# A decoder trunk on one core: giving out the splits of the weights with a lead of 6.0 instead of 4.0

## The chip, the cores and the metric

The kernel runs on one core of a Trainium2 chip. The metric is the device time of one execution in microseconds (us). The core has a matrix engine (TensorE: PE in the profile, with PEld for its weight loads), VectorE (DVE), ScalarE (ACT), GpSimd (POOL), SyncE (SP, which only issues transfers here), and 16 DMA engines. Each engine has one stream of instructions and works through it in order; semaphores make one engine wait for another.

## What is computed

Two layers of a hybrid decoder on 256 tokens of width 1024, in fp32 (`rms_norm`, `swiglu` and the sub-layers are the usual ones):

```python
for l in range(2):
    h = h + 0.5 * swiglu(rms_norm(h, ffn1_norm[l]), ffn1_w_gate[l], ffn1_w_up[l], ffn1_w_down[l])
    h = h + hybrid_mixer(rms_norm(h, mix_norm[l]), w_in[l], ...)      # S5 scan beside differential attention
    h = h + memory_cross_attention(rms_norm(h, xattn_norm[l]), rms_norm(mem, mem_norm[l]),
                                   xattn_wq[l], xattn_wkv[l], xattn_wo[l])
    h = h + 0.5 * swiglu(rms_norm(h, ffn2_norm[l]), ffn2_w_gate[l], ffn2_w_up[l], ffn2_w_down[l])
return rms_norm(h, final_norm)
```

The mixer projects once (`w_in`) into the scan's input and q, k, v; it runs a complex diagonal scan over the 256 tokens with a gated output (`w_glu`), and causal differential attention with a bias; both halves go through `w_out`.

## The kernel before

**Weights in two parts.** Every product is made of three matmuls: high part of the activations by high part of the weights, high by low, low by high. So each weight tile is split on the chip. A unit is a 128 x 1024 tile of weights. SP loads it into one of `N_RAW` = 4 buffers (tile `raw`, in `fetch`, L578). ScalarE makes the high part (`whi`, times a gain where the norm's gain is folded in), VectorE the low part (`wlo` = raw times gain minus `whi`). `split_unit` (L582) does so for one half of 512 columns at a time, `split_whole` (L525) for all 1024 in ffn2. High and low parts have `N_W` = 5 buffers each.

**The list of units.** `stream_plan` (L104) lists all units in the order of use, with `need`, the time of each unit's first use on a clock that counts TensorE's ticks on weights alone: `STEP` = 1.28 per unit and token block, so 2.56 from unit to unit of a plain projection, which uses each unit for both blocks of 128 tokens at once. At the seams of sub-layers (ffn1 and ffn2 at their ends, w_glu, w_out, wq, wo) four units are held together: first all four for block 0, then all four for block 1, while block 0 is already being finished. In ffn2 pairs of chunks are made with seven products each in the manner of Strassen; such a unit ("S") is used for one STEP only.

**What sets the order.** The order of every engine's instructions is set when the program is written, by a planner: `Clock` (L168) carries `now`, the time of TensorE, and the times until which ScalarE, VectorE and GpSimd are occupied, by costs per instruction. The main program emits the matmuls on weights. Everything else (evacuations, attention, scan, tables) runs as tasks, Python generators, which are put in a heap with the time at which their input should be ready. Before every three matmuls on one half of a unit the main program calls `tick` (L618):

```python
def tick(self, ready):
    self.feed()
    self.c.run_due()
    self.c.now = max(self.c.now, ready + 0.13)
    self.main += STEP / 2
```

First `feed` (L503) emits splits, then `run_due` (L219) emits the tasks that are due, then `now` is moved to the time at which the planner has the half ready, then `main`, the place of the stream, moves by 0.64. `feed` goes on until a half is too far ahead or the buffers are used up:

```python
u, q = divmod(self.nsplit, 2)
if u >= self.nfree + N_W or (u > least and self.need[u] + q * STEP / 2 > self.main + LEAD):
    break
```

`split_next` (L515) also emits the loads: that of unit u + 4 behind the split of unit u.

**The mixer** (L1324). TensorE runs the four chunks of `w_in` (16 units), three chunks of `wkv` (12 units, products with the memory tokens, which depend on nothing in the layer and are there to fill the time), then `w_glu` and `w_out`. Beside the units run as tasks: `ssm_evac` (L1339), which copies the scan's input from PSUM (tile `z`) and changes its layout by four transfers issued on ScalarE's queue (tile `uq`); `ssm_states` (L1368), which reads `uq` into `up`, transposes it, and does the rotations and the scan on VectorE (tiles `p`); `attn` (L1478) for each token block, with its scores, maxima (`nm`) and sums on VectorE (tiles `sb`); and `ssm_out` (L1439), matmuls on the scan's result (`acc` from `W` and `p`). `w_glu` waits for its result.

Of the kernel before, what the change touches and what calls it, by code (L numbers as in the profile page):

```python
# [33 lines left out]
N_W = 5  # L34
N_S4 = 12
N_T5 = 3
LEAD = 4.0
STEP = 1.28
MARGIN = 0.2
BURST = 0.8  # L40
# [320 lines left out]
class Trunk:  # L361
# [141 lines left out]
    def feed(self, least=-1):  # L503
# [4 lines left out]
        while self.nsplit < 2 * n:  # L508
# [3 lines that stand above are left out]
# [1428 lines left out]
```

## Time and profile before

| | |
|---|---|
| median of 3 runs | 1204.16 us (1203.55 to 1204.84) |
| the profiled execution | 1206.8 us, its span 1203.7 us |
| TensorE matmuls busy | 1187.4 us (99%) |
| TensorE weight loads busy | 971.2 us (81%) |
| VectorE busy | 903.1 us (75%) |
| ScalarE busy | 711.2 us (59%) |
| bytes moved, mean rate | 210.91 MB, 175 GB/s |
| granted TensorE clock | 0.999 of full speed |

The profile is of one execution. Matmuls are pipelined, and their ends are modelled, so the distance between the starts of two matmuls tells more than their durations. A group of instructions carries the line of the helper that emits them (L345 matmuls, L356 transposes, L269 VectorE, L306 ScalarE), so groups are told apart by their tiles.

### The profile page before, as it was taken

To read this page: it belongs to the slowest core of one execution; us is meant where nothing else is said; L and a number is where in the kernel's file an instruction comes from. 1 tells how busy PE (TensorE), PEld (TensorE's weight loads), DVE (VectorE), ACT (ScalarE), POOL (GpSimd) and SP (SyncE) were. 2 spreads that over 40 slices of the span, in tenths; PEclk is the share of its full clock that TensorE was granted. 3 is DMA by queue.
4 is the path that set the end of the run, shared out by engine and by line. 5 is a ranking of instruction groups with operands and counts; after the bars stand their busy time and mean duration, and the time that the engine had idled before them with its cause. 6 is when DMAs were issued, how large, how long until landed. Compare 5 with 4: busy or idle time off the path is not lost.

```text
span 1203.7 us, 17730 instructions
## 1 busy us (share of the span) xinstructions
PE 1187.4 (99%) x6580; PEld 971.2 (81%) x6580; DVE 903.1 (75%) x1498; ACT 711.2 (59%) x1206; POOL 45.1 (4%) x104
## 2 busy tenths in 40 slices
PE   8999999999999999999999999999999999999997
PEld 7888888777888888888888888887678888888886
DVE  5797776498866688978668878565978576788885
ACT  6665455556856566555465544555687665556553
POOL 2100001000000000000010000100000000000000
PEclk9999999999999999999999999999999999999999
DMA  8656455544544566473556655655436455746542
GB/s 272 216 183 200 159 174 173 172 123 141 193 158 140 157 222 217 132 265 128 175 193 191 191 162 177 184 167 150 139 123 197 155 156 174 297 124 222 189 136 83
DMA packets 59974, 210.91 MB, mean 175 GB/s; under 512 B 7168, under 2 KB 8288, under 8 KB 59888
## 3 DMA queue, kind: packets, MB, share of 16 engines
q1 hardware_dynamic: 56304, 202.92, 51.8%
q0 software_dynamic: 2000, 5.24, 1.4%
q10 hardware_dynamic: 1584, 1.62, 0.5%
q8 instruction: 51, 0.84, 0.3%
q14 instruction: 35, 0.29, 0.1%
HBM read 207.00 MB, written 1.05 MB: 173 GB/s over the span
## 4 chain that ended last, share of the span: by engine, by line
PE 94%; DVE 2%; DMA 2%; ACT 1%; issue 1%; ACTq 0%; POOLq 0%; POOL 0%; DVEq 0%
PE mm L345 48%; PE acc L345 33%; PE tp L345 8%; PE tp L356 5%; DMA uq<-z 1%; DVE wlo L269 1%; DVE p L269 1%; DMA h<-in_x 0%; ACT whi L306 0%; DVE nm L269 0%; ACT junk L306 0%; ACT z L306 0%; ACT up L306 0%; ACTq L315 0%; DVE h L269 0%
## 5 line engine op out<-in xcount | busy, mean ns | idle before, releaser
L269 DVE SCALAR_TENSOR_TENSOR wlo<-raw,gains,whi 128x512 fp32r<-128x512 f32 x368 | 263.0, 747 | 92.2 <-ACT whi L306 90.7
L345 PE MATMUL mm<-whi,xh 128*128 128x512 f32 x768 | 307.0, 400 | 0.0
L345 PE MATMUL mm<-whi,xl 128*128 128x512 f32 x768 | 300.0, 391 | 0.0
L345 PE MATMUL mm<-wlo,xh 128*128 128x512 f32 x768 | 299.3, 390 | 0.3 <-DVE wlo L269 0.3
L306 ACT ACTIVATE whi<-raw,gains 128x512 fp32r<-128x512 f32 x368 | 240.8, 713 | 14.9 <-DMA raw<-in_wst 6.6
L345 PE MATMUL acc<-whi,gT 128*128 128x512 f32 (+1 forms) x712 | 238.9, 396 | 0.0
L269 DVE TENSOR_TENSOR wlo<-raw,whi 128x512 fp32r<-128x512 f32 (+1 forms) x236 | 209.7, 911 | 20.9 <-ACT whi L306 19.7
L306 ACT ACTIVATE whi<-raw 128x512 fp32r<-128x512 f32 (+1 forms) x236 | 180.9, 805 | 45.0 <-DMA raw<-in_wst 21.4
L345 PEld LDWEIGHTS mm<-whi,xh 128*128 128x128 f32 x768 | 144.5, 188 | 31.4 <-issue 1.3
L345 PEld LDWEIGHTS mm<-whi,xl 128*128 128x128 f32 x768 | 144.3, 188 | 30.6
L345 PEld LDWEIGHTS mm<-wlo,xh 128*128 128x128 f32 x768 | 144.8, 189 | 28.0 <-DVE wlo L269 0.6
L345 PEld LDWEIGHTS acc<-whi,gT 128*128 128x128 f32 x712 | 133.2, 188 | 26.3
L345 PE MATMUL acc<-wlo,gT 128*128 128x512 f32 (+1 forms) x356 | 138.0, 388 | 0.0
L345 PE MATMUL mm<-whi,mem 128*128 128x512 f32 x256 | 92.6, 410 | 0.0
L345 PEld LDWEIGHTS acc<-wlo,gT 128*128 128x128 f32 x356 | 67.1, 189 | 11.7
L306 ACT ACTIVATE sg<-mm,rstd 128x256 f32<-128x256 f32 x44 | 20.9, 474 | 85.5 <-PE mm L345 85.4
L306 ACT ACTIVATE gT<-tp 128x512 fp32r<-128x512 f32 x44 | 26.3, 598 | 56.4 <-PE tp L356 56.4
L306 ACT ACTIVATE z<-mm,rstd 128x256 f32<-128x256 f32 (+1 forms) x52 | 29.7, 571 | 49.6 <-PE mm L345 48.8
L345 PEld LDWEIGHTS mm<-whi,mem 128*128 128x128 f32 x256 | 48.1, 188 | 11.4 <-issue 1.3
L345 PE MATMUL mm<-wlo,mem 128*128 128x512 f32 x128 | 51.0, 398 | 3.9 <-DVE wlo L269 3.9
L306 ACT ACTIVATE xh<-tp 128x512 fp32r<-128x512 f32 x32 | 19.1, 596 | 59.6 <-PE tp L356 59.6
L269 DVE TENSOR_TENSOR gT<-tp,gT 128x512 fp32r<-128x512 f32 x44 | 30.2, 687 | 21.7 <-ACT gT L306 21.7
(256 smaller groups left out, 1539.9 us busy)
## 6 DMA issues: line engine op xcount, KB each, us to landing
raw<-in_wst SPq DMA_DIRECT2D x350, 512.0 KB, 4.0
blkX<-in_wst SPq DMA_DIRECT2D x8, 512.0 KB, 4.6
blkP<-in_wst SPq DMA_DIRECT2D x8, 512.0 KB, 8.1
blkY<-in_wst SPq DMA_DIRECT2D x8, 512.0 KB, 8.9
blkQ<-in_wst SPq DMA_DIRECT2D x8, 512.0 KB, 9.6
raw<-in_wst SPq DMA_DIRECT2D x4, 256.0 KB, 5.7
mem<-in_mem POOLq DMA_DIRECT2D x2, 512.0 KB, 7.4
uq<-z ACTq DMA_DIRECT2D x8, 128.0 KB, 4.7
```

The source lines that it names most:

```text
L269: r = getattr(self.e, name)(*a, **k)
L306: r = self.e.activation(out, in_, func, **k)
L345: r = self.e.matmul(out, lhsT, rhs, **k)
L356: r = self.e.transpose(out, in_, ident)
```

## The change

One constant of `feed` is changed: a half may be given out when it is needed within 6.0 of the stream's place instead of 4.0. The number of buffers, the list of units, the costs and everything else stay.

```diff
 N_W = 5
 N_S4 = 12
 N_T5 = 3
-LEAD = 4.0
+LEAD = 6.0
 STEP = 1.28
 MARGIN = 0.2
 BURST = 0.8
```

## Rows read from the trace of the kernel before

**Rows 1.** Page, part 1: engine, busy us, share of the span, instructions.

```profile
PE 1187.4 (99%) x6580; PEld 971.2 (81%) x6580; DVE 903.1 (75%) x1498; ACT 711.2 (59%) x1206; POOL 45.1 (4%) x104
```

**Rows 2.** Page, part 4: the chain that ended last, shares by engine.

```profile
PE 94%; DVE 2%; DMA 2%; ACT 1%; issue 1%; ACTq 0%; POOLq 0%; POOL 0%; DVEq 0%
```

**Rows 3.** Waits of TensorE, whole span: waited for, us in total, times, longest.

```profile
PE mm L345 <- DVE wlo L269: 4.2, 5, 1.4
...
PE tp L356 <- ACT up L306: 1.5, 2, 0.8
```

**Rows 4.** The same in two stretches: 262 to 275 us, then 855 to 868.

```profile
PE mm L345 <- DVE wlo L269: 2.0, 2, 1.4
...
PE mm L345 <- DVE wlo L269: 1.9, 2, 1.4
```

**Rows 5.** Windows view: stretch, length, then busy us and instructions of each engine.

```profile
241.00:292.00 51.00, 49.02 (x340) 36.39 (x338) 49.34 (x79) 31.17 (x70) 0.00 (x0) 1.00 0.44 135
```

**Rows 6.** Undisturbed matmuls (chain), then TensorE's timeline: start, us, instruction, count, [idle before].

```profile
316.52 16.33 PE acc L345 x72
...
264.81 0.62 PE L345 MATMUL mm<-whi,mem 128*128 128x512 f32 x2
...
267.17 0.62 PE L345 MATMUL mm<-whi,mem 128*128 128x512 f32 x2
...
269.22 0.62 PE L345 MATMUL mm<-whi,mem 128*128 128x512 f32 x2
...
270.21 0.63 PE L345 MATMUL mm<-whi,mem 128*128 128x512 f32 x2
...
272.28 0.62 PE L345 MATMUL mm<-whi,mem 128*128 128x512 f32 x2
...
273.81 0.63 PE L345 MATMUL mm<-whi,mem 128*128 128x512 f32 x2
...
275.66 0.39 PE L345 MATMUL mm<-wlo,mem 128*128 128x512 f32 x1
```

**Rows 7.** VectorE's timeline in the same stretch.

```profile
263.76 1.22 DVE L269 TENSOR_TENSOR p<-p,rot 128x1023 f32<-128x1023 f32 x1
...
266.03 0.75 DVE L269 SCALAR_TENSOR_TENSOR wlo<-raw,gains,whi 128x512 fp32r<-128x512 f32 x1
...
267.94 1.21 DVE L269 TENSOR_REDUCE nm<-sb 128x4 f32<-128x1024 f32 x1
269.07 1.41 DVE L269 SCALAR_TENSOR_TENSOR wlo<-raw,gains,whi 128x512 fp32r<-128x512 f32 x2
270.40 1.22 DVE L269 TENSOR_TENSOR p<-p,rot 128x1023 f32<-128x1023 f32 x1
...
272.67 2.07 DVE L269 SCALAR_TENSOR_TENSOR wlo<-raw,gains,whi 128x512 fp32r<-128x512 f32 x3
```

**Rows 8.** Timelines of VectorE and TensorE: two results and the instructions that use them.

```profile
276.03 0.35 DVE L269 SCALAR_TENSOR_TENSOR sb<-sb,sums 128x128 f32<-128x128 f32 x1
...
276.80 0.38 PE L356 MATMUL tp<-ident,sb 128*128 128x128 f32 x2
...
280.26 1.22 DVE L269 TENSOR_TENSOR p<-p 128x1023 f32<-128x1023 f32 x1
...
285.98 0.41 PE L345 MATMUL acc<-W,p 64*64 64x64 f32 x16
```

**Rows 9.** Chain of the stretch at the mixer's entry; then uq's times to landing.

```profile
218.83 1.93 ACT whi L306 x3
...
220.81 0.70 ACT z L306
...
222.14 6.22 DMA uq<-z
...
DMA to landing us min/median/max: 3.0/4.7/6.6
```

**Rows 10.** Page, part 6: issues, count, KB each, median us to landing.

```profile
raw<-in_wst SPq DMA_DIRECT2D x350, 512.0 KB, 4.0
```

## What to expect of it, worked out before it ran

> **What bounds the kernel now.** I read the page's busy shares first: TensorE has 1187.4 us of matmuls in a span of 1203.7 [rows 1]. The chain of work that ended last says the same from the other side: 94% of it is TensorE, 2% VectorE, 2% DMA [rows 2]. So whatever a change of order can give back is in the few places where TensorE waits. The waits of TensorE name them: 4.2 us for low halves of weights (tile wlo) in five waits, and 1.5 us for the tile up in two [rows 3]. Asked by stretch, four of the five waits for wlo are in two short stretches, one per layer, 2.0 and 1.9 us [rows 4]: the first units of wkv in the mixer, where VectorE also runs the scan of the SSM and the softmax of the attention. VectorE is busy for 49.3 of 51 us there [rows 5]. The late halves are not late because work is missing on ScalarE or from memory, but because they stand behind other instructions in VectorE's queue.
>
> **The change, part by part.** It removes and adds no instruction. The same units are loaded, split and multiplied; only the places in the instruction streams move. Four things move with LEAD.
>
> *When a half is given out.* feed issues half q of unit u at the first tick at which need[u] + 0.64 q is no more than main + LEAD, and main grows by 0.64 a tick. Units of a plain projection are four ticks apart. Counted from a unit's own first tick, its two halves are given out at ticks -6 and -5 with 4.0 (4.0/0.64 = 6.25) and at -9 and -8 with 6.0 (9.375): three ticks earlier. A tick is three matmuls; 72 of them take 16.33 us [rows 6], so 0.227 us each, 0.68 us a tick, 2.04 us for the three. Where a group of four is held for both token blocks, the limit of N_W = 5 buffers cuts this to about one to two ticks; the mixer's stretch is plain projections, so it gets all three.
>
> *What the late halves cost today.* Matmuls are paced by their starts, so I take starts, not the idle column, which misses part of it. Three matmuls take 0.68 us undisturbed. From the pair at 264.81 to the pair at 267.17 they took 2.36, from 269.22 to 270.21 0.99, from 272.28 to 273.81 1.53 [rows 6]. The excess is 1.68 + 0.31 + 0.85 = 2.84 us. The second layer repeats the pattern with a wait of 1.9 where this one has 2.0 [rows 4]; I take 2.8 for it too. Full removal is worth 5.6 us, and no more can come from this cause.
>
> *Whether three ticks are enough.* The three late halves are second halves of the first three wkv units. The first ends after the row at 266.03, behind two rotations of the scan that began at 263.76; the second is the first of the two at 269.07, behind a maximum that began at 267.94; the third is the first of the three at 272.67, behind two more rotations from 270.40 [rows 7]. Each was given out in the tick after, or a few ticks after, the scan step in front of it, so three ticks put it ahead of that step: 2.27 us earlier (263.76 to 266.03), 1.13 (267.94 to 269.07), 2.27 (270.40 to 272.67). Needed on a TensorE that never waited: about 1.7, 1.9 and 2.7. So at least the first is cured, the others nearly.
> The bound from below comes from the next unit. Its first half is the second of the three at 272.67 and ends near 274.1; it is used at 275.66 today [rows 6, 7], which would be 272.83 on a TensorE 2.83 us ahead. If it passes no scan step, 1.25 us of the gain is given back there, and a mixer yields 1.6. The bound from above is the full 2.8.
> I take 2.35 per mixer, nearer the upper end, for this reason: steps of the scan are put into the stream when the kernel's own clock says that the last one is done, and that clock is held up by a late weight (tick takes the weight's ready time into it). That it follows the chip through these waits is seen behind them: the first transposes of the attention's weights start at 276.80, 0.42 us after their input ends (276.03 + 0.35) [rows 8], although TensorE had lost 2.84 us just before. With less waiting, more ticks pass per scan step, and the next unit's halves pass the rotations too. Sum: 2 x 2.35 = 4.7 us.
>
> *What is pushed back instead.* The scan and the attention then finish later by what passed them: one and a half halves (three ticks of a half's two) and some two more where TensorE catches up, 0.7 us each by the spacing of the three at 272.67 [rows 7], so 1 to 2.5 us. The cover: the last rotation ends at 281.48 (280.26 + 1.22) and the matmuls on its result start at 285.98 [rows 8], 4.5 us; with TensorE 2.35 earlier and the scan 1 to 2 later it is nearly used up, not overdrawn. If it were gone, each us shows as a wait of the matmuls acc on W and p.
>
> *Queues that are passed.* ScalarE gives the high halves out three ticks earlier too; its evacuations (z, sg, xh, gT, qs) then stand behind up to two more halves, but most of them find ScalarE waiting for TensorE, so the halves fit into that idle time. SP's loads move with the splits: a slot is free earlier and its 512 KB, 4.0 us to landing [rows 10], are asked for earlier, at the same rate. The one DMA issue on ScalarE that matters is uq, below. POOL's few instructions are passed by nothing. All this I cost at 0, with plus or minus 0.7 us per mixer for uq (its wait today is 0.7 to 0.8 [rows 3]).
>
> *A rule that speaks against it.* TensorE's matmuls fill 99% of the span [rows 1]. The Trainium skill ("Perfetto Trace Analysis", Identifying the Most-Contended Engine) tells to improve the engine with the highest occupancy first; by that, reordering VectorE's queue would change nothing and the sum would be 0. The same section warns that the matmuls' busy share is a poor measure of TensorE. The starts above agree with the warning: inside rows that count as busy, 0.2 to 0.4 us per late half is lost beyond the idle column.
>
> **Against the runs.** The profiled execution took 1206.8 us, its span 1203.7. 1206.8 - 4.7 = 1202.1. That execution lies 2.6 above the median of the runs, 1204.16; on the scale of the medians the forecast is 1199.5. Differences under 0.2%, 2.4 us, can't be told from no change.
>
> **The rivals.**
> *The wait moves.* If the order on TensorE around the scan and the attention stays as it is, TensorE comes to the transposes of sb 2.8 us earlier, and these have 0.42 us to spare [rows 8]; 2.4 of 2.8 us come back as waits there. Gain 0.4 per mixer: 1203.4, at worst 1204.2. For it: VectorE has hardly a free microsecond [rows 5], so somebody has to be late. Against it: that clock reacts, and the streams have other units to run meanwhile.
> *The change doesn't do what it says.* The halves are given out earlier but VectorE's order in the crowded stretch stays, since scan steps come in blocks of two and a shift of three ticks may fall between two blocks; and elsewhere five buffers cap it. Then nothing moves: 1204.2, within 0.5. For it: one of the three late halves passes only 1.13 us of work. Against: the other two pass 2.27.
> *Slower: the exchange uq.* At the mixer's entry the chain runs through ScalarE: halves whi from 218.83, the copy z at 220.81, then the transfer uq from 222.14, 6.22 us long [rows 9], and TensorE waits for up at its end. It has no cover at all: every microsecond later goes through from the first one on. Two more halves in front of z cost 1.3 us (1.93/3 each) [rows 9]; one more weight load in front of uq costs up to the 4.0 us that a load takes to land [rows 10]. Both together are 5.3 us per mixer, 10.6 in all: 1204.16 - 4.7 + 10.6 = 1210.1. It ends above 1206.6 from 3.6 us per mixer on. For it: uq's time to landing already spreads from 3.0 to 6.6 us [rows 9]. Against: by the tick count only three or four halves fall between the two copies z instead of four, and the last copy waits for TensorE anyway.
> The Trainium skill says ("DMA: Bandwidth & Descriptors", Issuing engines are not separate DMA queues) that transfers from all issuing engines run on the same 16 DMA engines and interleave; by that uq is slowed by the weight loads beside it. The spread of uq agrees with it, though it doesn't prove it.
>
> **How the numbers follow.** Forecast 0.58, at 1199.5; its own range is 1204.16 - 5.6 - 0.8 = 1197.8 to 1204.16 - 3.2 + 0.8 = 1201.8. The wait moves 0.17, at 1203.4. Nothing changes 0.11, at 1204.2. Slower through uq 0.14, at 1210, the near end of it at 1206.6. The range of 1197.8 to 1206.2 leaves out most of the last case and some hundredths below. Faster by over 0.2% is the forecast but for its upper edge, 0.57; the same is the two middle cases and that edge, 0.29; slower is 0.14.
>
> **What would show it.** Right: TensorE's waits for wlo between 262 and 275 and between 855 and 868 fall from 2.0 and 1.9 us to under 0.5; in VectorE's timeline of that stretch the second half of the first wkv unit stands ahead of the two rotations; the last rotation ends a little later against the start of wkv; the rest of the span is as long as it was. Wrong: the waits for wlo are gone and as much appears at the transposes of sb or the matmuls on W (the wait moved); VectorE's order is unchanged (no effect); or the stretch from the copy z to up is longer by some us (uq). A gain over 6 us would mean that weights were late in places that the waits don't show.

## The result, and the profile after

The changed kernel takes 1213.24 us (median of 4 runs, 1212.84 to 1214.25) where the kernel before took 1204.12 beside it: a ratio of 1.0077, 95% interval 1.0064 to 1.0090, so 9 us slower. The forecast was 1199.5. The profiled execution took 1213.41, its span 1211.6 against 1203.7, 7.9 us more, at a granted clock of 0.997 against 0.999.

The first and the fourth part of the page after (busy time of each engine; shares of the chain that ended last), which answer [rows 1, 2]:

```profile
PE 1188.9 (98%) x6580; PEld 971.5 (80%) x6580; DVE 904.1 (75%) x1498; ACT 710.7 (59%) x1206; POOL 44.7 (4%) x104
...
PE 91%; ACT 4%; DVE 2%; issue 2%; DMA 1%; POOL 0%; ACTq 0%; POOLq 0%; DVEq 0%
```

Every count of instructions is what it was. Busy time is the same within 1.5 us on every engine. What changed is the chain: TensorE has 3% less of it, ScalarE 4% instead of 1%. TensorE's waits after (waited for, us in total, times, longest), which answer [rows 3]:

```profile
PE tp L356 <- DVE vl L269: 4.2, 4, 1.5
PE tp L345 <- DVE yT L269: 3.7, 2, 1.8
PE mm L345 <- DVE z L269: 2.4, 4, 0.8
PE tp L356 <- DVE prob L269: 2.0, 2, 1.0
...
PE mm L345 <- DVE wlo L269: 0.3, 1, 0.3
```

The waits that the change aimed at are gone: wlo fell from 4.2 to 0.3, and none is left in the two stretches of [rows 4] (the 0.3 is in the opening, at 14.9 us, and was there before); the two waits for up [rows 3] are gone too. In their place stand four others, each once or twice per layer, and none of them is on a weight. They are on results that VectorE makes: yT (the scan's output, at 304 and 900 us), vl (w_out's input behind its gate, four times), prob (the cross attention's weights, at 393 and 991) and z (in ffn2, four times).

Measured as the prediction measured, by the distance between the starts of neighbouring matmuls beyond their usual distance (0.227 us for 128 x 512), the ledger of the span is:

| place | before | after |
|---|---|---|
| wlo in wkv, two layers | 5.6 | 0 |
| up, two layers | 1.8 | 0 |
| yT | 0 | 4.0 |
| vl | 0 | 4.9 |
| prob | 0 | 2.3 |
| z in ffn2 | 0 | 3.1 |

About 7.4 us were gained and 14.3 lost, in places that the prediction didn't look at. Two more items belong to the sum: the opening is 1.0 us shorter in this execution (the 100th matmul starts at 24.84 us, and at 25.81 before), and the clock cost 1.7.

**A price behind a wait.** In the second layer the granted clock falls right behind the wait for yT, which ended at 902.51. The windows view (stretch, length, busy us and instructions of PE, PEld, DVE, ACT and POOL, granted clock, DMA share, GB/s):

```profile
902.83:906.25 3.42, 3.42 (x16) 3.02 (x14) 2.40 (x4) 0.35 (x1) 0.00 (x0) 0.50 0.60 207
```

0.50 is the lower of TensorE's two levels, 1.2 GHz. Matmuls of 128 x 512 start 0.43 us apart there (904.54 and 904.97) instead of 0.227, so half of the 3.42 us, 1.7, is lost. Ahead of the fall TensorE had stood for 1.83 us. The first layer's wait, just as long, was followed by no fall, and the kernel before has no such stretch between its opening and its last matmul. So a wait can cost more than its own length.

**Where a new wait comes from.** VectorE's and TensorE's timelines, kernel after (start, us, instruction, count, [idle before and what ended it]), around prob, then around yT and z:

```profile
391.89 1.89 DVE L269 TENSOR_TENSOR wlo<-raw,whi 128x512 fp32r<-128x512 f32 x3 [0.66 <-ACT whi L306]
...
393.89 0.62 DVE L269 TENSOR_SCALAR prob<-prob,sums 128x256 f32<-128x256 f32 x2
...
394.39 0.63 PE L356 MATMUL tp<-ident,prob 128*128 128x128 f32 x4 [1.00 <-DVE prob L269]
...
303.43 0.74 DVE L269 SCALAR_TENSOR_TENSOR wlo<-raw,gains,whi 128x512 fp32r<-128x512 f32 x1
304.10 1.28 DVE L269 TENSOR_TENSOR wlo<-raw,whi 128x512 fp32r<-128x512 f32 x2
305.30 1.06 DVE L269 TENSOR_TENSOR yT<-tp,yT 128x512 fp32r<-128x512 f32 x1
...
306.41 1.16 PE L345 MATMUL tp<-z,aT 128*128 128x128 f32 x8 [1.83 <-DVE yT L269]
...
434.79 2.36 DVE L269 TENSOR_TENSOR wlo<-raw,whi 128x1024 fp32r<-128x1024 f32 x2 [0.47 <-ACT whi L306]
437.06 0.48 DVE L269 SCALAR_TENSOR_TENSOR z<-mm,rstd,z 128x256 f32<-128x256 f32 x1
```

Three halves of wo stand ahead of prob, 1.89 us of work that is not needed yet, while TensorE stands for prob. The kernel before has the same instructions the other way round:

```profile
391.86 0.62 DVE L269 TENSOR_SCALAR prob<-prob,sums 128x256 f32<-128x256 f32 x2
392.38 1.89 DVE L269 TENSOR_TENSOR wlo<-raw,whi 128x512 fp32r<-128x512 f32 x3
```

At yT it is a late half of wkv (gains) and two halves of w_glu (no gains), at z two units of ffn2. At vl there is one step more; ScalarE's, VectorE's and TensorE's timelines, kernel after:

```profile
320.36 2.70 ACT L306 ACTIVATE whi<-raw,gains 128x512 fp32r<-128x512 f32 x4 [1.61 <-PE acc L345]
...
324.37 0.63 ACT L306 ACTIVATE gt<-gt 128x512 f32<-128x512 f32 x1
...
325.65 1.41 DVE L269 SCALAR_TENSOR_TENSOR wlo<-raw,gains,whi 128x512 fp32r<-128x512 f32 x2 [1.76 <-ACT whi L306]
326.98 0.68 DVE L269 TENSOR_TENSOR vl<-vl,gt 128x512 f32<-128x512 f32 x1
...
330.02 0.63 PE L356 MATMUL tp<-ident,vl 128*128 128x128 f32 x4 [1.54 <-DVE vl L269]
```

ScalarE first stands 1.61 us, until matmuls of TensorE end, before it can make four high halves; the sigmoid gt, which vl needs, waits behind them and a table load of 1.28 us; on VectorE two more halves stand ahead of vl. ScalarE's idle time ahead of whi, by what ended it (us, times), gives the size of that for the whole kernel, first before, then after:

```profile
  PE acc L345: 17.0, 13
...
  PE mm L345: 4.1, 4
```

```profile
  PE acc L345: 55.6, 27
  PE mm L345: 18.0, 13
```

21.1 us before, 73.6 after. Nothing but a buffer can make a split wait for a matmul, since its input comes from memory: `feed` counts a buffer as free when its last matmul has been emitted, and a half given out that early stands at the head of ScalarE's queue until the chip has done that matmul. Whatever is queued behind it stands too. That this costs TensorE time is tried in the third experiment.

### The profile page after: what moved, and what is told of

It is laid out like the page before. It is cut to its first block, busy times and chain, and to the rows that moved or that the text cites. A ratio compares the mean times of both kernels' runs of the same rounds, so it can differ in the third digit from the quotient of the medians.

```text
span 1211.6 us, 17723 instructions
## 1 busy us (share of the span) xinstructions
PE 1188.9 (98%) x6580; PEld 971.5 (80%) x6580; DVE 904.1 (75%) x1498; ACT 710.7 (59%) x1206; POOL 44.7 (4%) x104
## 4 chain that ended last, share of the span: by engine, by line
PE 91%; ACT 4%; DVE 2%; issue 2%; DMA 1%; POOL 0%; ACTq 0%; POOLq 0%; DVEq 0%
PE mm L345 47%; PE acc L345 31%; PE tp L345 8%; PE tp L356 5%; DVE wlo L269 1%; ACT whi L306 1%; ACT junk L306 1%; ACT L306 1%; DMA h<-in_x 0%; ACT xh L306 0%; DMA raw<-in_wst 0%; DVE vl L269 0%; ACT yg L306 0%; DVE yT L269 0%; POOL rstd L329 0%
## 5 line engine op out<-in xcount | busy, mean ns | idle before, releaser
L306 ACT ACTIVATE whi<-raw,gains 128x512 fp32r<-128x512 f32 x368 | 243.6, 714 | 45.5 <-PE acc L345 32.1
L269 DVE SCALAR_TENSOR_TENSOR g<-mm,rstd,sg 128x256 f32<-128x256 f32 x44 | 21.1, 481 | 39.3 <-ACT sg L306 39.3
```

The costliest lines, as they stand in the source:

```text
L269: r = getattr(self.e, name)(*a, **k)
L306: r = self.e.activation(out, in_, func, **k)
```

## The experiments

The theory after the result: the halves of the *next* group stand ahead of evacuations for which TensorE is about to wait (order), and a part of it is ScalarE standing for a buffer (buffers). Rivals: the mixer itself pays, because the scan was pushed back; or the earlier transfers disturb. In each experiment but the third, fourth and sixth, `feed` takes the lead from a function of the unit's group, and the diff shows that function, with its constants written out (from the seventh on against the function of an earlier experiment):

```diff
-self.need[u] + q * STEP / 2 > self.main + LEAD
+self.need[u] + q * STEP / 2 > self.main + lead_of(self.plan[u])
```

Times are medians beside runs of the kernel before on the same chip (1204.2 to 1204.8).

**1. The mixer's stretch alone.**

```diff
+def lead_of(p):
+    return 6.0 if p[0] == "w_in" or (p[0] == "wkv" and p[2] < 12) else 4.0
```

> The lead of 6.0 for the mixer's projections alone (w_in and the three chunks of wkv in it), 4.0 for all other units. What the comparison of the traces suggests: the longer lead takes away the waits of TensorE for wlo in wkv (5.6 us by starts, both layers) and for up (1.8), and the new waits (yT 4.0, vl 4.9, prob 2.3, z 3.1 us by starts) each have halves of the NEXT group's units in front of them: w_glu before yT, w_out and wq before vl, wo before prob, ffn2 before z. By that theory this run keeps the gain and drops vl, prob and z: 1196.5 to 1201 us, the upper end if yT's wait stays. The rival, that the shift of the mixer itself sets its tail off balance (TensorE comes out of wkv 8 us earlier than before, at results that are no earlier), gives waits for yT and vl here too: 1203 to 1208 us.

Measured: 1197.64 us, ratio 0.9937 (0.9920 to 0.9954); span 1197.2. TensorE's waits have one new row, for yT (1.3 us, twice, 0.7 at most), and none for vl, prob, z, up. So the change is worth 6.5 us of span (7.2 by the medians) where the prediction looked, even more than forecast, and the wait for yT, 0.8 us per layer by starts, is all that the scan's tail pays for it.

**2. All but the mixer's stretch.**

```diff
+def lead_of(p):
+    return 4.0 if p[0] == "w_in" or (p[0] == "wkv" and p[2] < 12) else 6.0
```

> The complement: 4.0 for w_in and the mixer's wkv, 6.0 for all other units. Theory of the next group's halves: waits for wlo in wkv are back (5.6 us), vl, prob and z stay (10.3 us), yT with them in part: 1212 to 1219 us. Rival (mixer off balance): prob and z stay (5.4 us), vl and yT go: 1207 to 1211 us.

Measured: 1215.92 us, ratio 1.0090 (1.0075 to 1.0105); span 1213.8. TensorE's waits:

```profile
PE mm L351 <- DVE wlo L275: 4.1, 5, 1.4
PE tp L362 <- DVE vl L275: 2.8, 4, 0.8
PE mm L351 <- DVE z L275: 2.4, 4, 0.8
PE tp L362 <- DVE prob L275: 2.0, 2, 1.0
```

The waits of before are back (up, with 1.3, is further down), and vl, z and prob are there without the mixer: the loss comes from the other groups. A wait for g in the opening, 1.8 us, is in this run and not in the whole change. The halves don't add: -6.5 and +10.1 us of span make +3.6, the whole made +7.9. By starts and without the first 25 us, where the opening differs, the gap is 5.3 us, and three items make it up: yT loses 2.0 us per layer by starts in the whole change and 0.8 in the first experiment, vl's first wait 1.7 against 1.0 in this one, and the clock cost 1.7 in the whole and nothing in either half. At a seam, halves of both groups meet.

**3 and 4. Buffers or order.** Six buffers for the parts, while `feed` is still held to five units, so that no half is given out earlier; the space comes from N_S4 (another pool, 12 to 10). The control has the smaller pool alone. Both have the lead 6.0 everywhere.

```diff
 N_W = 5
+N_BUF = 6
-N_S4 = 12
+N_S4 = 10
...
-        self.hip = P("hi", N_W)
-        self.lop = P("lo", N_W)
+        self.hip = P("hi", N_BUF)
+        self.lop = P("lo", N_BUF)
```

> Lead 6.0 everywhere, halves given out by the same limits (five units), but six buffers each for high and low parts, paid for with two of the twelve general tiles (10 instead of 12). With the longer lead ScalarE stands at a split whose buffer TensorE has not left for 89 us instead of 27, and holds what is behind it. If these stand-stills cause the new waits (theory of the buffers), they go here: 1199 to 1206 us. If only the place in the queue counts (a half in front costs its own 0.7 us on ScalarE and on VectorE, waiting or not), the time stays at that of the changed kernel: 1211 to 1215 us.

> Control for the run with six buffers: lead 6.0, five buffers, ten general tiles instead of twelve. Both theories: the changed kernel's time within 1.5 us, 1211.5 to 1215 us; if it is slower, that is the price of the two tiles and is to be taken off the run with six buffers.

Measured: six buffers 1208.24 us, ratio 1.0031 (1.0020 to 1.0042), span 1206.0; the control 1213.62, ratio 1.0071 (1.0056 to 1.0086), span 1210.5, with the waits of the changed kernel. Neither profile has a stretch at the lower clock in mid-span, so the 4.5 us between the two spans hold nothing of the clock. TensorE's waits, and ScalarE's idle time for TensorE ahead of whi, six buffers:

```profile
PE tp L346 <- DVE yT L270: 3.7, 2, 1.8
PE mm L346 <- DVE z L270: 2.4, 4, 0.8
PE tp L357 <- DVE prob L270: 2.0, 2, 1.0
...
PE tp L357 <- DVE vl L270: 0.5, 2, 0.2
```

```profile
  PE acc L346: 5.4, 10
```

With a buffer to spare ScalarE stands 5.4 us instead of 73.6, and vl falls from 4.9 us by starts to 0.8. yT, z and prob keep their size to a tenth. So about 4 us of the loss is ScalarE standing for buffers, and it shows at vl alone; the other 9.4 us (4.0 + 2.3 + 3.1) stay, and by the timelines above they are plain order on VectorE. The fifth experiment tries that.

**5. Three groups put back to 4.0.** w_glu, wo and ffn2 go back to 4.0; w_in, wkv, wq, w_out and ffn1 keep 6.0.

```diff
+def lead_of(p):
+    return 4.0 if p[0] in ("w_glu", "wo", "ffn2_gu", "ffn2_dn") else 6.0
```

> Lead 6.0, but 4.0 for the units of w_glu, wo and ffn2, whose halves stand in front of yT, prob and z in the changed kernel. Theory of the place in the queue: these three waits go (4.0 + 2.3 + 3.1 us by starts), vl stays (4.9), since it hangs on the buffers: 1213.3 - 9.4 = 1203.9, so 1202 to 1206 us. Rival (the waits come from TensorE's being early at the mixer's tail, and from ScalarE's time in general): yT or prob stay for the most part: 1207 to 1211 us.

Measured: 1203.74 us, ratio 1.0000 (0.9990 to 1.0009); span 1201.9. prob (wo stood ahead of it) and z (ffn2) are gone, vl is unchanged at 4.2, a wait for g in the opening has 1.3, yT is down from 3.7 to 1.3, as in the first experiment. Each of the three waits goes, or shrinks to what the first experiment has, with the group whose halves stand ahead of it.

**6. A lead of 5.0 everywhere.**

```diff
-LEAD = 6.0
+LEAD = 5.0
```

> Half of the change: lead 5.0 everywhere. By the rounding to ticks a half of a plain projection is given out one tick earlier than with 4.0 (at -7 for -6), not three. If gain and loss both grow with the lead step by step: TensorE's waits for wlo in wkv fall by about half (2 to 3 us less), and part of the new waits (vl, yT, prob, z) is there, 3 to 7 us: 1204 to 1209 us. If the loss sets in at once where halves come to stand in front of an evacuation, it is all there already: 1210 to 1214 us.

Measured: 1215.66 us, ratio 1.0093 (1.0078 to 1.0108); span 1214.4. Halfway between is slower than either end, for two reasons of its own. The first is a wait for z, once per layer, 8.9 us in total. ScalarE's timeline and TensorE's:

```profile
290.48 1.28 ACT L306 ACT_TABLE_LOAD   x1
291.77 1.09 ACT L306 ACTIVATE yg<-acc 128x512 f32<-128x512 f32 x2
...
295.10 1.28 ACT L306 ACT_TABLE_LOAD   x1
296.40 0.51 ACT L306 ACTIVATE sb<-sb,nm 128x256 f32<-128x256 f32 x1
...
301.28 1.23 ACT L306 ACTIVATE z<-mm,rmem 128x512 f32<-128x512 f32 x2
...
301.99 0.79 PE L345 MATMUL mm<-whi,mem 128*128 128x512 f32 x1 [4.43 <-ACT z L306]
```

Here the scan's gelu (yg) has come to stand ahead of the exponentials of the attention's second block (sb) on ScalarE, with a table load of 1.28 us ahead of each; in the kernel before the exponentials come first (290.27) and one load (294.84) lies between them and yg. All this, and yT, stands ahead of z, which frees the PSUM tile that TensorE needs: ScalarE works without a pause from 288.85 to the end of z. There are 13 table loads in the kernel where before and after have 11. The second reason is the clock. It is at its lower level at both waits, for 6.83 us from 301.19 and for 3.41 from 901.93, which is worth 5.1 us; all four runs have a mean clock of 0.993 to 0.995. By this estimate 5.0 would take about 1210.5 us at the full clock, and 6.0, without its 1.7, about 1211.5. The lead doesn't only shift halves: it changes which ticks pass while a task waits, and with that the order of the tasks among each other.

**7 and 8. Other leads around a mixer at 6.0.** First everything else at 3.0, then w_glu alone at 3.0 with the rest at 4.0.

```diff
 def lead_of(p):
-    return 6.0 if p[0] == "w_in" or (p[0] == "wkv" and p[2] < 12) else 4.0
+    return 6.0 if p[0] == "w_in" or (p[0] == "wkv" and p[2] < 12) else 3.0
```

```diff
 def lead_of(p):
+    if p[0] == "w_glu":
+        return 3.0
     return 6.0 if p[0] == "w_in" or (p[0] == "wkv" and p[2] < 12) else 4.0
```

> Lead 6.0 for the mixer's projections, 3.0 for all others (two ticks less than before). Outside of the mixer the weights had 1.1 us or more to spare with 4.0 except at the first units of ffn2 (0.4 to 0.6 us). If a shorter lead only takes spare time away, little changes or waits for wlo at the groups of four appear: 1197 to 1201 us. If evacuations still stand behind halves at 4.0, less lead is a gain: 1195 to 1197 us.

> Lead 6.0 for the mixer's projections, 3.0 for w_glu, 4.0 for the rest: the run with the mixer alone, but with w_glu's halves moved further back from yT. If the wait for yT that is left there (0.8 us by starts in each layer) comes from w_glu's halves in front of it, it goes: 1195.5 to 1197 us; if from TensorE's earlier arrival, nothing moves: 1197 to 1198.5 us.

Measured: 1207.32 us, ratio 1.0025 (1.0015 to 1.0036), and 1201.01 us, ratio 0.9973 (0.9962 to 0.9984). Both are slower than expected. A shorter lead brings weights late: with 3.0 the matmuls of w_glu wait 1.8 us for wlo in both, and with 3.0 everywhere there are 2.1 us more of waits for wlo in other groups and 0.9 for z in ffn2. The wait for yT (1.3) doesn't move with w_glu's lead: without w_glu's halves it is one half of wkv itself that stands ahead of yT (302.67 and 303.33 on VectorE).

**9. The mixer's wkv alone.**

```diff
 def lead_of(p):
-    return 6.0 if p[0] == "w_in" or (p[0] == "wkv" and p[2] < 12) else 4.0
+    return 6.0 if p[0] == "wkv" and p[2] < 12 else 4.0
```

> Lead 6.0 for the mixer's three chunks of wkv alone, 4.0 for w_in and the rest. The run with w_in and wkv at 6.0 won 7.2 us and lost the waits for wlo in wkv (5.6 us by starts) and for up (1.8). If the wait for up goes by w_in's halves being out of the way of the copy z and the transfer uq, it is back here: 1198.5 to 1200.5 us. If it went for another reason, 1197 to 1198.5 us.

Measured: 1203.49 us, ratio 0.9992 (0.9983 to 1.0002); span 1201.3. Neither expectation held. The waits for wlo are mostly gone, as expected, but the wait for up stays, and yT is larger than in the first experiment:

```profile
PE tp L362 <- DVE yT L275: 3.3, 2, 1.6
PE tp L362 <- ACT up L312: 1.7, 2, 1.3
```

**10. w_in and two of the three chunks of wkv.** If the half ahead of yT is one of the last chunk, that chunk should go back to 4.0.

```diff
 def lead_of(p):
-    return 6.0 if p[0] == "w_in" or (p[0] == "wkv" and p[2] < 12) else 4.0
+    return 6.0 if p[0] == "w_in" or (p[0] == "wkv" and p[2] < 8) else 4.0
```

> Lead 6.0 for w_in and the first two chunks of wkv, 4.0 for the third chunk and the rest. With all three chunks at 6.0 one wait for yT of 0.8 us per layer is left, behind one half of wkv's last unit on VectorE. If that half is the cause, the wait goes and the time falls by 1 to 1.6 us: 1195.8 to 1197 us. If TensorE only comes too early there, it stays: 1197.2 to 1198.5 us.

Measured: 1196.85 us, ratio 0.9937 (0.9920 to 0.9953); span 1195.0, the shortest of all. All of TensorE's waits:

```profile
PE pz L351 <- DVE zero L275: 1.2, 1, 1.2
PE tp L362 <- DMA h<-in_x: 0.7, 1, 0.7
PE mm L351 <- DVE wlo L275: 0.3, 1, 0.3
```

What is left lies in the first 16 us. Against the first experiment its time is not distinguishable: the medians differ by 0.8 us, and of the 2.2 us between the profiled spans 1.7 lie in the opening, where the two kernels give out the same halves (its wait for wlo ends at 16.24 us in the first experiment and at 14.54 here).

The wait for yT is gone, but not for the reason expected. Two halves of wkv still stand just ahead of yT on VectorE (from 303.46 us; yT starts at 304.78). What has changed is TensorE's order: the second group of transposes of yg starts 4.8 us behind the first (301.68 and 306.45) and not 1.14 us behind it (303.04 and 304.18 in the first experiment), so matmuls on wkv lie between the two. The expected time came by another way than the expected one, and whether the half of the last chunk was the cause stays open.

**11 and 12. Its two parts, each alone.** What does w_in's lead do, and do the parts add?

```diff
 def lead_of(p):
-    return 6.0 if p[0] == "w_in" or (p[0] == "wkv" and p[2] < 8) else 4.0
+    return 6.0 if p[0] == "w_in" else 4.0
```

```diff
 def lead_of(p):
-    return 6.0 if p[0] == "w_in" or (p[0] == "wkv" and p[2] < 8) else 4.0
+    return 6.0 if p[0] == "wkv" and p[2] < 8 else 4.0
```

> Only the units of w_in are given out with 6.0, everything else with 4.0. In e8 (the mixer's wkv alone with 6.0) TensorE's wait for up was still there, 0.6 and 1.4 us by starts, while with w_in at 6.0 too it is gone. Theory that the longer lead of w_in itself removes it: the wait for up is gone here (-1.8 us), the four waits for wlo in wkv stay (5.6 us by starts), no wait for yT, vl, prob or z beyond those of before: 1202.4, range 1201.6 to 1203.4. Rival, that the wait for up goes only when w_in and wkv are moved together: up stays, 1204.2.

> Only the first two chunks of the mixer's wkv are given out with 6.0, w_in and the rest with 4.0. Theory that the parts add: against the version with w_in and two chunks (1196.85) it misses what w_in's lead gives, the wait for up (2.0 us in e8) and 0.9 us of wlo at wkv's first unit: 1199.8, range 1199 to 1200.8, with no wait for yT, since the third chunk's halves stand where they stood. Rival, that the waits for yT in e8 (3.6 us) came from w_in at 4.0 beside wkv at 6.0 and not from the third chunk: they stay, 1203.4.

Measured: 1207.63 us, ratio 1.0025 (1.0015 to 1.0035), and 1206.38, ratio 1.0013 (1.0004 to 1.0022). Each part alone is slightly slower than before; together they are 7 us faster. Much of that slowness is the clock. With w_in alone it is at its lower level twice, from 296.90 and from 890.82, each time right behind the wait for yT; the first stretch:

```profile
296.90:300.32 3.42, 3.42 (x12) 2.86 (x11) 2.94 (x8) 2.18 (x10) 0.00 (x0) 0.50 0.50 153
```

The two are worth 3.4 us, and all nine runs of this kernel have a mean clock of 0.994 to 0.997 where the kernel before has 0.998 to 0.999. The twelfth run's profile has one such stretch (from 900.02), 1.7 us. Without them, by estimate, each part alone would take about the time of the kernel before.

The first theory is half right: with w_in at 6.0 the wait for up is gone in every run here, with 4.0 it stays (1.3 to 1.7 us). But both have a wait for yT, 2.9 and 2.2 us per layer by starts, that neither theory had in it. TensorE's waits, w_in alone, then ScalarE's timeline and VectorE's ahead of the first of them:

```profile
PE tp L351 <- DVE yT L275: 5.4, 2, 2.7
```

```profile
290.25 1.28 ACT L312 ACT_TABLE_LOAD   x1
291.55 0.51 ACT L312 ACTIVATE sb<-sb,nm 128x256 f32<-128x256 f32 x1
...
294.15 1.06 ACT L312 ACTIVATE yT<-tp 128x512 fp32r<-128x512 f32 x1
...
295.24 1.07 DVE L275 TENSOR_TENSOR yT<-tp,yT 128x512 fp32r<-128x512 f32 x1 [0.21 <-ACT yT L312]
```

Here the exponentials and a table load stand between the transposes and their evacuation. In the twelfth run it is the attention's norms and two halves that do, and both transposes of yg come at once, so that the two evacuations follow each other. With both parts, and in the kernel before, the two groups of transposes are 3.8 to 4.8 us apart and neither evacuation holds TensorE; in every run here that waits for yT they start within 1.2 us of each other.

## Why the prediction was wrong

**Bound and mechanism: right.** The late halves stood behind the scan's steps in VectorE's queue, and an earlier place cures them. The second half of the first wkv unit started 1.68 us after the first matmul of wkv (266.03 and 264.35) and starts 2.52 us before it now; the kernel after, VectorE, then TensorE's first matmul of wkv, answering [rows 6, 7]:

```profile
259.95 0.74 DVE L269 SCALAR_TENSOR_TENSOR wlo<-raw,gains,whi 128x512 fp32r<-128x512 f32 x1
260.62 1.22 DVE L269 TENSOR_TENSOR p<-p,rot 128x1023 f32<-128x1023 f32 x1
...
278.44 1.22 DVE L269 TENSOR_TENSOR p<-p 128x1023 f32<-128x1023 f32 x1
...
262.47 0.39 PE L345 MATMUL mm<-whi,mem 128*128 128x512 f32 x1
...
284.62 0.41 PE L345 MATMUL acc<-W,p 64*64 64x64 f32 x16
```

It passed both rotations, as foretold. The term was taken at 4.7 us out of 5.6; all of it came, and VectorE is as busy there as it was (49.16 of 51 us, against 49.34 in [rows 5]).

**What is pushed back: priced too high.** The last rotation ends 17.19 us after wkv's first matmul (278.44 + 1.22 - 262.47), and ended 17.13 after it before; its cover before the matmuls on W is 4.96 us, and was 4.50 [rows 8]. The 1 to 2 us charged to it were not paid. "The wait moves" didn't happen at sb either.

**uq: mis-sized, and for a reason not thought of.** Priced at plus or minus 0.7 us per mixer, it gave 0.9 per layer. Not because uq came sooner (the median to landing near the first mixer is 6.3 us, and was 4.7), but because the planner now puts the transposes of up later into TensorE's stream: 16.79 us after the transposes of h (229.17 - 212.38) where it was 14.75 (229.58 - 213.96, less the 0.87 lost there). The rival that ends on the slower side gave a time near the one measured, by a mechanism that went the other way; that is no point for it.

**The failed step: "Queues that are passed ... All this I cost at 0".** Its reason was that "most of them find ScalarE waiting for TensorE, so the halves fit into that idle time". Two things are wrong with it. It weighs ScalarE alone, while three of the four places where TensorE came to wait (yT, prob and z) hang on VectorE's own order, which beyond the scan and the attention stands in no term; prob and z lie outside the mixer, and LEAD governs all units of the kernel. The second experiment, without the mixer, shows +10.1 us of span. And idle time on an engine says nothing about the one instruction for which TensorE waits next: a half of 0.63 to 0.74 us ahead of an evacuation holds it, however idle the engine is over the stretch. It needed the price that was given to uq: so many halves by 0.7 us, at every seam where TensorE needs an evacuation with little to spare. At prob three halves are 1.89 us and cost 1.15 per layer; at yT 0.8 is lost with one half of wkv ahead and 2.0 with two of w_glu's as well. A term for the clock, which fell behind one of these waits and took 1.7 us, was missing too. The remark that groups of four are "cut to about one to two ticks" by five buffers treated the limit as a shield. The third experiment shows it as a cost: the limit of five lets a half out when its buffer is not free on the chip, and ScalarE stands at it, 4 us of TensorE's time.

**The rule weighed there.** The Trainium skill ("Perfetto Trace Analysis", Identifying the Most-Contended Engine) tells to optimize the engine with the highest occupancy first. The prediction read from it that order on VectorE, 75% busy, would be worth nothing; the section doesn't say that. The runs disagree with that reading: with the same instructions, order moves the time from 1196.85 to 1215.92 us (tenth and second experiment), and what it moves are waits of TensorE, the engine with the highest occupancy (98 to 99%).

**Against the marks set.** "The rest of the span is as long as it was" is the mark that failed; the other three (wlo under 0.5, the half ahead of the rotations, the last rotation a little later, by 0.06 us) were met.

**What stays open.** That the waits come from the groups outside the mixer, that vl's hangs on the buffers, and that prob, z and most of yT go with wo, ffn2 and w_glu, is shown by the first, second, third and fifth experiment; what is left at yT is read from timelines only. Which order the planner makes from a given lead was not foretold in the last four experiments, and the version with w_in and two chunks owes its place to the way its tasks happen to fall at yT. Why one wait is followed by a lower clock and another is not was not tried. That the earlier transfers as such cost something was not tried by itself; the tenth experiment, with earlier transfers in the mixer, has no such wait.

## What to carry to other kernels

A lead of prefetch is a place in the queues of the engines that prepare the data, so look at each seam at the instruction just behind the moved one, and at who waits for it; the lead belongs to a group of weights, not to the kernel. Here 6.0 for w_in and the first two chunks of wkv with 4.0 for all else makes 1196.85 us, while 6.0 for all makes 1213.24. Where a planner counts a buffer as free when its last reader is emitted, an early split holds everything behind it until that reader has run.

## What the runs showed that was not expected

The measured time is not monotonic in the lead: 1204.1 us at 4.0, 1215.7 at 5.0, 1213.2 at 6.0, of which the clock has about 5.1 at 5.0 and 1.7 at 6.0; and parts that are slower each (1207.6, 1206.4) make a whole that is faster (1196.9), of which the clock has 3.4 and 1.7 in the profiled executions. A granted clock of 0.50 for 3.4 to 6.8 us came at or right behind some of TensorE's waits of 1.8 us and more, so the time of a wait is not its whole price. Two loads of ScalarE's function table per layer, 1.28 us each, stand in the unbroken run of ScalarE's work that ends in a wait of 4.4 us.
